# Bulk weights of the second layer through ScalarE's queue, late weights asked for two steps later, the first output tile's load three steps ahead, the keys' sums in another pool

## The chip, the core and the metric

One core of one Trainium2 chip runs the whole kernel. TensorE (PE) multiplies matrices; VectorE (DVE), ScalarE (ACT) and GpSimd (POOL) work on tiles in SBUF and read results from PSUM; SyncE (SP) does nothing but issue transfers. ScalarE can issue transfers too: SPq and ACTq in the profile are the two issuing queues. The metric is the device time of one execution in microseconds, the median of several.

## The reference

A prompt of 2048 tokens and a sample of 64 tokens go through two layers with 16 heads of 64. Layer A is softmax attention over a band of chunks, layer B is "stick-breaking" attention over a K/V pair that is projected from A's output. Cut to what matters:

```python
h = rms_norm(x, norm_a)
q, k, v, gate = split(h @ w_in_a, 4)
x = x + (band_attend(q, k, v, rel_bias) * silu(gate)) @ w_out_a     # layer A
k, v = split(rms_norm(x, norm_kv) @ w_kv, 2)                         # shared K/V
q, gate = split(rms_norm(x, norm_b) @ w_in_b, 2)
x = x + (sb_block(q, k, v) * silu(gate)) @ w_out_b                   # layer B
y = rms_norm(x, norm_f)

def sb_block(q, k, v):
    z = q @ k.T * SCALE
    log_fail = where(mask, log_sigmoid(-z), 0)
    later = suffix sums of log_fail, without the own place
    return where(mask, exp(log_sigmoid(z) + later), 0) @ v
```

Outputs are y for prompt and sample, and the new rows of K and V. Everything is f32.

## The kernel before, in words

To keep f32 accuracy, each operand is split into a high and a low part (names that end in h and l: `lwh`, `lwl`, `ph`, `pl`, `oh`, `ol`), and a product is two or three matmuls into one PSUM bank.

Each layer is a projection stage, bound by matmuls, and an attention stage. In the attention stage TensorE makes scores (`z`), transposes weights (`wt<-ident,s`) and multiplies by V (`acc<-ph,vt`, `acc<-pl,vt`); ScalarE makes exponentials and sigmoids (`f<-z`) and copies (`ph<-wt`), VectorE and GpSimd do the rest (`s`, `two`, `pl`). Results go to DRAM through `ot` (two buffers) as `o_a` and `o_b`.

Beside the attention, the class `Beat` puts in steps of other matrix work from a list, `beside`, at a rate of 0.4 (A) or 0.3 (B) steps a beat, so that TensorE has something to do while others work on the scores. The list holds, in order:

- late projections (`job_steps`, `late_job`): the second half's keys in layer A (8 jobs), the second half's gates (`w_bg`) and queries (`w_bq`) in layer B (16 jobs). A job has weights (`lwh`, `lwl`, from DRAM in layer B, where they were split before; in A split on the spot from `lraw`), eight products (`ps_j`, two chunks of four steps) and what follows: `sg` through ScalarE for gates, `sp` for queries and keys. For keys, `add_back` sums the two parts on GpSimd (`lkn<-sp`) and `token_rows` turns them for the output.
- `w_out_steps`, eight steps of one entry: layer A loads `woraw` and splits it into `big`; layer B loads the parts from DRAM, where they lie split (`parts`, 16 loads `big<-wo` of 512 KB).
- `out_steps`: output tiles of 128 tokens. Each loads `og` (o times gate) and `xr` (the residual), splits og into `oh` and `ol` in two cuts, and has eight products `ps_o`.

An entry is a triple: what to do ahead (loads, cuts), products, and what goes behind. `Beat.step` takes one product of the current entry per call. At an entry's first step it asks for the next entry's load; in the second half of the current entry it spreads the next entry's cuts. An entry whose load was not asked for waits nine beats after it (`ready`).

The order on an engine is Tile's scheduler's, except for what `in_place` pins: a pinned instruction stays behind the one traced before it on the same engine. Late weights, bulk weights and output tiles' loads are pinned. All transfers named here go through SyncE in the kernel before (`sp.dma_start`); ScalarE's queue carries loads of `wraw` and a few stores in the projection stages only. Transfers take eight completion semaphores in turn, over both queues, and an issue waits for the transfer eight issues earlier.

The pools that the change names: `lpool` and `rpool` lie on the two sides of SBUF, and a tile waits for the last readers of what lay in its place. `opool` has two buffers each of `oh` and `ol` (late weights and cuts share them), two of `xr` (also `sg` and `sp`), one of `og` (also `lraw`). PSUM tag `wt` (three banks) holds `wt` and `ps_j`.

In the profile almost every engine instruction has one line, that of the helper `traced` (L90), so instructions are told apart by their tiles.

Of the kernel before, what the change touches and what calls it, by code (L numbers as in the profile page):

```python
# [21 lines left out]
NP = 2048  # L22
# [26 lines left out]
HOLD = dict(a=1, b=2)  # L49

STEP = 2

SETTLE = 5
TOK = [(t * P, min(P, T - t * P)) for t in range((T + P - 1) // P)]
# [46 lines left out]
def encoder_step(ctx: ExitStack, tc: tile.TileContext, a: dict, o: dict):  # L101
# [634 lines left out]
    def late_job(L, kind, w, c0, g, hp, x2, first, prompt, rows_pool):  # L736
        st = {}

        def load():
            if L not in KEPT:  # L740
                st["raw"] = opool.tile([P, NK, P], F32, name="lraw", tag="og", bufs=1)
                c = c0 + hp * P
                sp.dma_start(st["raw"], w[:, c : c + P].rearrange("(k p) c -> p k c", p=P))
            st["wh"] = opool.tile([P, NK, P], F32R, name="lwh", tag="oh", bufs=2)
            st["wl"] = opool.tile([P, NK, P], F32R, name="lwl", tag="ol", bufs=2)
            if L in KEPT:
                for i, part in enumerate((st["wh"], st["wl"])):
                    sp.dma_start(f32(part), f32(lay[L]["w"][kind, hp][i]))

        def cut(k0):  # L750
            ks = slice(k0, k0 + STEP)
            scaled_split(st["wh"][:, ks], st["wl"][:, ks], st["raw"][:, ks], g[:, ks])

        def some(c, k0):
            if k0 == 0:
                st["ps"] = bank("ps_j")
            ps, wh, wl = st["ps"], st["wh"], st["wl"]
            cols = slice(c, c + CH)
            for k in range(k0, k0 + STEP):
                mm(ps, wh[:, k], x2[0][:, k, cols], start=(k == 0), stop=False)  # L760
                mm(ps, wh[:, k], x2[1][:, k, cols], start=False, stop=False)
                mm(ps, wl[:, k], x2[0][:, k, cols], start=False, stop=(k == NK - 1))

        def out(c):
            ps = st["ps"]
            at = slice(place(HALF + c), place(HALF + c) + CH)
            if kind == "g":
                sg = opool.tile([P, CH], F32, name="sg", tag="xr", bufs=2)
                act.activation(sg, ps, AF.Sigmoid)
                dve.tensor_tensor(sg, ps, sg, ALU.mult)  # L770
                queue.store(lay[L]["g"][hp][:, at], sg)
            else:
                sp = opool.tile([P, 2, CH], F32R, name="sp", tag="xr", bufs=2)
                split(sp[:, 0], sp[:, 1], ps)
                for s in range(2):
                    put(L, kind, hp, s, at, sp[:, s], queue.store)
                st[c] = sp
            if c + CH == HALF:
                done_late.add((L, kind, hp))

        def add_back(c):

            st["kn"] = rows_pool.tile([P, CH], F32, name="lkn", tag="lkn", bufs=1)
            gps.tensor_tensor(st["kn"], f32(st[c][:, 0]), f32(st[c][:, 1]), ALU.add)

        def token_rows(c):
            kn = st["kn"]
            ps = bank("ps_r")
            for j in range(4):
                flip(ps[:, j * P : j * P + P], kn[:, j * P : j * P + P])  # L790
            act.activation(kn, ps, AF.Copy)
            b = HALF + c - first
            dst = prompt[b : b + CH, hp * P : hp * P + P]
            queue.store(dst.rearrange("(j p) c -> p j c", p=P), kn.rearrange("p (j c) -> p j c", j=4))

        chunks = range(0, HALF, CH)
        behind = []
        for c in chunks:
            rows = kind == "k" and HALF + c >= first
            behind.append([partial(out, c)] + ([(2, partial(add_back, c)), (4, partial(token_rows, c))] if rows else []))  # L800
        products = [partial(some, c, k0) for c in chunks for k0 in range(0, NK, STEP)]
        cuts = [] if L in KEPT else [partial(cut, k0) for k0 in range(0, NK, STEP)]
        return [in_place(x) for x in [load] + cuts], products, behind

    def w_out_steps(src, w):

        raws = {}

        def parts(k):
            if k == 0:  # L810
                w.extend(big_pair())
            for i in range(2):
                sp.dma_start(f32(w[i][:, k]), f32(wod[k][:, i]))

        if src is None:
            return [([], [None], [[in_place(partial(parts, k))]]) for k in range(NK)]

        def load(k):
            if k < NK:
                tag = ("oh", "ol")[k % 2]  # L820
                raws[k] = opool.tile([P, D], F32, name="woraw", tag=tag, bufs=2)
                sp.dma_start(raws[k], src[k * P : (k + 1) * P])

        def cut(k):
            if k == 0:
                w.extend(big_pair())
            for c in range(0, D, CH):
                cols = slice(c, c + CH)
                split(w[0][:, k, cols], w[1][:, k, cols], raws[k][:, cols])
            del raws[k]  # L830

        return [
            (
                [in_place(partial(load, i)) for i in range(3)] if k == 0 else [],
                [None],
                [[in_place(partial(cut, k)), in_place(partial(load, k + 3))]],
            )
            for k in range(NK)
        ]
# [60 lines left out]
    class Beat:  # L900
# [4 lines left out]
        def __init__(self, lag, hold, scores_first, blank):  # L905
# [2 lines left out]
            self.clock = 0  # L908
            self.tiles, self.blocks, self.held, self.rests = [], [], [], []
            self.beside, self.rate, self.due = [], 0.0, 0.0  # L910
            self.now, self.at, self.ready, self.started = None, 0, 0, False
            self.steps, self.waiting = 0, []
            self.marks = []

# [9 lines left out]
        def step(self):  # L924


            if self.now is None:
                self.now, self.at = self.beside.pop(0), 0
                ahead = self.now[0]
                if ahead and not self.started:  # L930

                    ahead.pop(0)()
                    self.ready = self.clock + 9
                self.started = False
            if self.clock < self.ready:
                return 0.0
            ahead, products, behind = self.now
# [10 lines left out]
            n, rest = len(products), []  # L948
            half = max(n // 2, 1)
            following = self.beside[0][0] if self.beside else []  # L950
            if self.at == 0 and following:
                rest.append(following.pop(0))
                self.started = True
            self.at += 1
            if self.at % half == 0:
                for x in behind[self.at // half - 1]:
                    if type(x) is tuple:
                        self.waiting.append((self.steps + x[0], x[1]))
                    else:
                        rest.append(x)  # L960
            if self.at > half or n == 1:
                m = -(-len(following) // (n - self.at + 1))
                rest += [following.pop(0) for _ in range(m)]
            self.later(rest)
# [122 lines left out]
    with (  # L1087
# [8 lines left out]
        new = Sample("a", wpool)  # L1096
        w_out = []
        beat = Beat(LAG["a"], HOLD["a"], True, 1.0)
        beat.beside = job_steps("a", jobs_a, x2, NP - CACHE_A, o["a_k_p"], lpool)
        beat.beside += w_out_steps(a["w_out_a"][0], w_out)  # L1100
        order.on = False

# [161 lines left out]
    with (  # L1264
# [42 lines left out]
        new = Sample("b", wpool)  # L1307
        w_out = []
        beat = Beat(LAG["b"], HOLD["b"], False, 1.0)
        beat.beside = job_steps("b", jobs_b, x2, 0, o["b_k_p"], lpool)  # L1310
        beat.beside.insert(1, end_values())
        beat.beside += w_out_steps(None, w_out)
        order.on = False
# [235 lines left out]
```

## Time and profile before

| what | value |
|---|---|
| runs | 3270.53, 3279.95, 3283.12 us |
| median | 3279.95 us |
| profiled execution, own time | 3271.0 us |
| profiled execution, span | 3269.2 us |
| granted TensorE clock, mean | 0.996 |
| instructions | 53693 |
| DMA, moved over the span | 688.41 MB, 211 GB/s |

The span runs from the first to the last instruction; the execution's own time is 1.8 us longer. A row of a timeline has the start, the length, the engine, the line, the operation, its tiles (out<-in), their shapes and how many in a row, then in brackets the idle time of the engine before it and what ended that. PEld is TensorE's loading of the stationary operand, which lies beside the matmuls. A row of the windows has the busy time of each engine (and its instructions), then the granted clock (1.00 is full), the share of time in which the 16 DMA engines were busy (over 1 means that transfers overlap on them), and GB/s.

Layer A's attention runs from about 670 to 1420 us, layer B's from about 2030 us to the end. The late projections run at the start of each, `w_out_steps` of A around 980 to 1035 us, of B around 2650 to 2700 us.

### The profile page before, as it was taken

How to read it: one execution, taken by the hardware profiler on the slowest of the kernel's cores; microseconds unless marked ns; L12 is line 12 of the kernel's file. 1: busy time of each engine (PE TensorE's matmuls, PEld its weight loads, DVE VectorE, ACT ScalarE, POOL GpSimd, SP SyncE). 2: the span in 40 equal slices, each digit the busy share in tenths (PEclk: the TensorE clock that was granted, in tenths of full speed). 3: DMA queues.
4: the chain of work that ended last, by engine and by line, in shares of the span. 5: the costliest groups of instructions: out<-in, count | busy, mean ns of one | idle time of the engine just before them, and what ended most of it. 6: DMA issues, size and time to landing. Idle time of an engine off the chain costs nothing.

```text
span 3269.2 us, 53693 instructions
## 1 busy us (share of the span) xinstructions
PE 3198.9 (98%) x17928; PEld 2786.8 (85%) x17928; DVE 1882.2 (58%) x3786; ACT 1709.0 (52%) x3719; POOL 1291.7 (40%) x1950
## 2 busy tenths in 40 slices
PE   8999999999998999999999999999999989999999
PEld 7889999988887898878899999888888878888877
DVE  4235431147778776232044432888878878888873
ACT  5234222258888776143143442666666656666662
POOL 3001110025655554020044200444477767777761
PEclk9999999999999999999999999999999999999999
DMA  6359993387899983453399999977735575355423
GB/s 202 122 185 373 347 331 119 118 241 218 239 261 267 252 231 121 168 183 132 107 352 347 351 352 341 274 218 215 210 121 151 160 208 174 119 144 143 136 72 120
DMA packets 464891, 688.41 MB, mean 211 GB/s; under 512 B 51445, under 2 KB 261397, under 8 KB 464614
## 3 DMA queue, kind: packets, MB, share of 16 engines
q1 hardware_dynamic: 405158, 633.85, 62.1%
q10 hardware_dynamic: 59456, 51.13, 4.8%
q8 instruction: 143, 2.34, 0.3%
q14 instruction: 134, 1.10, 0.1%
HBM read 408.78 MB, written 276.07 MB: 209 GB/s over the span
## 4 chain that ended last, share of the span: by engine, by line
PE 77%; issue 7%; DVE 7%; DMA 4%; ACT 3%; POOL 2%; SPq 0%; POOLq 0%; ACTq 0%; DVEq 0%
PE ps_t L90 24%; PE ps_v L90 11%; PE acc L90 10%; PE z L90 9%; PE wt L90 9%; PE ps_j L90 7%; PE ps_o L90 5%; DVE s L90 3%; DVE pl L90 2%; PE ps_tr L90 1%; ACT ph L90 1%; DMA keys<-k_a 1%; ACT s L90 1%; DMA vt<-v_b 1%; PE ps_c L90 1%
## 5 line engine op out<-in xcount | busy, mean ns | idle before, releaser
L90 DVE TENSOR_TENSOR pl<-wt,ph 128x512 fp32r<-128x512 f32 (+1 forms) x864 | 552.4, 654 | 121.8 <-ACT ph L90 117.9
L90 ACT ACTIVATE ph<-wt 128x512 fp32r<-128x512 f32 (+1 forms) x864 | 485.5, 577 | 203.4 <-PE wt L90 181.9
L90 PE MATMUL ps_t<-x_own,wh 128*128 128x362 f32 (+1 forms) x2304 | 568.1, 327 | 0.0
L90 PE MATMUL wt<-ident,s 128*128 128x128 f32 x3472 | 550.6, 274 | 14.7 <-DVE pl L90 6.9
L90 PEld LDWEIGHTS wt<-ident,s 128*128 128x128 f32 x3472 | 417.2, 141 | 90.3 <-DVE pl L90 13.1
L90 ACT ACTIVATE f<-z 128x512 f32<-128x512 f32 (+4 forms) x680 | 355.0, 536 | 189.4 <-PE z L90 131.8
L90 PEld LDWEIGHTS ps_t<-x_own,wh 128*128 128x128 f32 x2304 | 405.4, 188 | 1.8
L90 POOL TENSOR_TENSOR s<-f,s 128x256 f32<-128x256 f32 x416 | 360.1, 867 | 104.0 <-DVE s L90 96.7
L90 PE MATMUL acc<-ph,vt 128*128 128x512 f32 (+3 forms) x1088 | 374.6, 379 | 17.8 <-ACT ot L90 8.6
L90 PE MATMUL z<-kt,q 128*128 128x512 f32 (+3 forms) x1280 | 373.6, 379 | 4.2 <-ACT f L90 2.7
L90 PE MATMUL ps_t<-x_own,wl 128*128 128x362 f32 (+1 forms) x1152 | 377.2, 328 | 0.0
L90 PE MATMUL acc<-pl,vt 128*128 128x512 f32 (+3 forms) x1088 | 363.3, 367 | 7.4 <-DVE pl L90 7.1
L90 POOL TENSOR_SCALAR s<-s,rc 128x640 f32<-128x640 f32 (+5 forms) x264 | 199.3, 759 | 387.8 <-DMA keys<-k_a 194.1
L90 PE MATMUL ps_o<-big,oh 128*128 128x512 f32 x1088 | 336.3, 393 | 0.0
L90 POOL TENSOR_TENSOR two<-f 128x256 f32<-128x256 f32 x416 | 258.7, 624 | 155.1 <-ACT f L90 139.8
L90 DVE TENSOR_TENSOR_SCAN s<-two,s,own 128x256 f32<-128x256 f32 x408 | 300.2, 739 | 34.2 <-POOL two L90 32.8
L90 PEld LDWEIGHTS z<-kt,q 128*128 128x128 f32 x1280 | 220.2, 190 | 33.8 <-ACT f L90 9.3
L90 PE MATMUL ps_j<-big,lwh 128*128 128x512 f32 x768 | 246.8, 397 | 1.5 <-DVE pl L90 0.6
L90 PE MATMUL ps_t<-big,wh 128*128 128x512 f32 x768 | 239.1, 392 | 0.0
L90 PEld LDWEIGHTS ps_o<-big,oh 128*128 128x128 f32 x1088 | 202.3, 188 | 40.9 <-ACT oh L90 0.2
L90 PEld LDWEIGHTS acc<-ph,vt 128*128 128x128 f32 x1088 | 197.4, 190 | 41.1 <-ACT ot L90 11.2
L90 DVE CUSTOM_DVE_ANT_0 s<-z,bias 128x640 f32<-128x640 f32 (+4 forms) x256 | 184.8, 733 | 78.5 <-PE wt L90 52.8
(148 smaller groups left out, 5526.7 us busy)
## 6 DMA issues: line engine op xcount, KB each, us to landing
vt<-v_b SPq DMA_DIRECT2D x80, 512.0 KB, 4.5
v_b<-vs SPq DMA_DIRECT2D x64, 512.0 KB, 5.9
q<-q_a SPq DMA_DIRECT2D x128, 256.0 KB, 5.9
q<-q_b SPq DMA_DIRECT2D x128, 256.0 KB, 4.3
vt<-v_a SPq DMA_DIRECT2D x48, 512.0 KB, 7.9
kt<-k_b SPq DMA_DIRECT2D x96, 256.0 KB, 5.6
keys<-k_a SPq DMA_DIRECT2D x80, 256.0 KB, 6.8
v_a<-vs ACTq DMA_DIRECT2D x32, 512.0 KB, 2.7
```

What stands on the lines that cost most here:

```text
L90: ins = op(*args, **kwargs)
```

## The change

Four edits:

1. The sums of the late keys (`lkn`) are allocated in `rpool` in place of `lpool`. Only layer A has them; in layer B the argument is without effect.
2. In layer B the loads of late weights (32) and of w_out's parts (16) are issued by ScalarE in place of SyncE.
3. An entry that has one thing to do ahead (layer B's late weights) is asked for at the third step of the entry before it (`BEHIND = 2`), in place of the first.
4. During `w_out_steps` (one product slot each), `step` looks up to three entries ahead for the first output tile and asks for its load then; where that tile is the very next entry, it waits nine beats and its cuts are not taken in at once. A name, `fetched`, holds which entry's load has been asked for, in place of the flag `started`.

```diff
+BEHIND = 2
...
             if L in KEPT:
                 for i, part in enumerate((st["wh"], st["wl"])):
-                    sp.dma_start(f32(part), f32(lay[L]["w"][kind, hp][i]))
+                    act.dma_start(f32(part), f32(lay[L]["w"][kind, hp][i]))
...
             for i in range(2):
-                sp.dma_start(f32(w[i][:, k]), f32(wod[k][:, i]))
+                act.dma_start(f32(w[i][:, k]), f32(wod[k][:, i]))
...
-                if ahead and not self.started:
+                if ahead and self.fetched is not ahead:
 
                     ahead.pop(0)()
                     self.ready = self.clock + 9
-                self.started = False
...
             following = self.beside[0][0] if self.beside else []
-            if self.at == 0 and following:
-                rest.append(following.pop(0))
-                self.started = True
+            coming = following
+            if n == 1:
+                coming = next((x[0] for x in self.beside[:3] if x[1] != [None]), [])
+            late = False
+            if coming and self.fetched is not coming and self.at == (BEHIND if n > 1 and len(coming) == 1 else 0):
+                rest.append(coming.pop(0))
+                self.fetched = coming
+                late = n == 1 and coming is following
+                if late:
+                    self.ready = self.clock + 9
...
-            if self.at > half or n == 1:
+            if self.at > half or n == 1 and not late:
...
-        beat.beside = job_steps("a", jobs_a, x2, NP - CACHE_A, o["a_k_p"], lpool)
+        beat.beside = job_steps("a", jobs_a, x2, NP - CACHE_A, o["a_k_p"], rpool)
...
-        beat.beside = job_steps("b", jobs_b, x2, 0, o["b_k_p"], lpool)
+        beat.beside = job_steps("b", jobs_b, x2, 0, o["b_k_p"], rpool)
```

How this moves instructions, at three places.

SyncE's queue, layer A, at the second half of the load of w_out (`woraw`). The names: `og` and `xr` are the first output tile's loads, `q`, `vt`, `gt` the attention's, `o_a` a store of its results. Before:

```order
L127 DMA o_a_109<-ot 128x512
L134 DMA gt<-gate_a_99 128x512
L134 DMA q<-q_a_82 64x2x512
L90 DMA woraw<-in_w_out_a 128x1024
L134 DMA q<-q_a_83 64x2x512 x2
L134 DMA vt<-v_a 128x4x256
L90 DMA woraw<-in_w_out_a 128x1024
```

and now:

```order
L128 DMA o_a_109<-ot 128x512
L135 DMA gt<-gate_a_99 128x512
L135 DMA q<-q_a_82 64x2x512
L91 DMA og<-o_a_107 128x8x128
L91 DMA xr<-in_x_prompt 128x1024
L91 DMA woraw<-in_w_out_a 128x1024
L135 DMA q<-q_a_83 64x2x512 x2
```

The two loads of the tile moved up by 22 rows, from behind a `vt` further down, past the second half of `woraw`, five loads of `vt` and the stores of `o_a_108`, `out_a_k_p` and `o_a_110`.

ScalarE, start of layer B's attention. The names: `lwh`/`lwl<-w_bq` are the second late job's weights, `<-w_bg_142` the third's, `sg` the first job's results (two chunks), `ends` a tile of the sample's, `f` scores. Before:

```order
L90 ACTIVATE kh<-ps_c 128x512
L90 ACTIVATE sh<-ps_t 128x362
L90 ACTIVATE kh<-ps_c 128x512
L90 ACT_TABLE_LOAD
L90 ACTIVATE sg<-ps_j 128x512 x2
L90 ACTIVATE ends<-ps_e 128x136
```

and now:

```order
L91 ACTIVATE sh<-ps_t 128x362
L91 DMA lwh<-w_bq_149 128x1024
L91 DMA lwl<-w_bq_149 128x1024
L91 ACTIVATE kh<-ps_c 128x512
L91 ACT_TABLE_LOAD
L91 ACTIVATE sg<-ps_j 128x512
L91 DMA lwh<-w_bg_142 128x1024
L91 DMA lwl<-w_bg_142 128x1024
L91 ACTIVATE sg<-ps_j 128x512
L91 ACTIVATE ends<-ps_e 128x136
```

The second job's weights now stand ahead of `kh`; the third's stand between the two `sg`.

SyncE, layer B, where the parts of w_out were loaded (`big`). Before:

```order
L90 DMA big_30644<-wo_165 128x1024
L90 DMA big_30645<-wo_165 128x1024
L90 DMA og<-o_b_137 128x8x128
L90 DMA xr<-x_158 128x1024
L134 DMA vt<-v_b 128x4x256
L90 DMA big_30644<-wo_166 128x1024
L90 DMA big_30645<-wo_166 128x1024
```

and now, the same place in the attention (`kt`, `q`, `vt` of the same block):

```order
L135 DMA kt<-k_b_122 64x2x512
L135 DMA vt<-v_b 128x4x256
L135 DMA kt<-k_b_122 64x2x512
L135 DMA q<-q_b_114 64x2x512
L135 DMA kt<-k_b_122 128x2x512
L135 DMA qs_21394<-q_b_116 64x2x64 x2
L135 DMA vt<-v_b 128x4x256 x5
```

The bulk loads have gone, and the first tile's `og` and `xr` stand earlier (behind the last stores of `q_b_118`'s first chunk and ahead of its second).

ScalarE, the same place now; before there was no DMA among these rows:

```order
L91 ACTIVATE otmp<-total_21401 64x64 x2
L91 DMA big_30644<-wo_160 128x1024
L91 DMA big_30645<-wo_160 128x1024
L91 ACTIVATE f<-z 128x512
L91 DMA big_30644<-wo_161 128x1024
L91 DMA big_30645<-wo_161 128x1024
L91 ACTIVATE ph<-wt 128x512 x3
L91 ACTIVATE f<-z 128x512 x2
L91 ACTIVATE ph<-wt 128x512
L91 ACTIVATE f<-z 128x512 x2
L91 DMA big_30644<-wo_162 128x1024
L91 DMA big_30645<-wo_162 128x1024
```

The pairs stand between ScalarE's `f` and `ph`, one pair for each step of `w_out_steps`.

More of the change, by code (lines that the diff above doesn't have):

```diff
@@ L910, in __init__ @@
             self.beside, self.rate, self.due = [], 0.0, 0.0
-            self.now, self.at, self.ready, self.started = None, 0, 0, False
+            self.now, self.at, self.ready, self.fetched = None, 0, 0, None
             self.steps, self.waiting = 0, []
```

## The prediction

> **What bounds the kernel now.** I read the page first: its busy shares, and the chain that ended last.
>
> ```profile
> span 3269.2 us, 53693 instructions
> PE 3198.9 (98%) x17928; PEld 2786.8 (85%) x17928; DVE 1882.2 (58%) x3786; ACT 1709.0 (52%) x3719; POOL 1291.7 (40%) x1950
> PE 77%; issue 7%; DVE 7%; DMA 4%; ACT 3%; POOL 2%; SPq 0%; POOLq 0%; ACTq 0%; DVEq 0%
> ```
>
> TensorE is busy for 3198.9 of 3269.2 us, and the change takes no matmul away. So all that it can win lies in 3269.2 − 3198.9 = 70.3 us of idle time, and in what the clock loses behind an idle stretch. The next view is therefore TensorE's waits, by what ended them (total, times, longest). I keep the rows that the change can touch.
>
> ```profile
> PE acc L90 <- ACT ot L90: 8.6, 4, 6.0
> PE acc L90 <- DMA vt<-v_b: 8.1, 2, 5.4
> PE wt L90 <- POOL s L90: 5.1, 4, 4.4
> PE z L90 <- ACT f L90: 2.7, 7, 1.0
> PE ps_j L90 <- DMA lwl<-w_bq: 1.2, 1, 1.2
> PE ps_j L90 <- DMA lwh<-w_bq: 0.5, 1, 0.5
> ```
>
> Five of the six are one long wait each with little beside it: single places, each with its own cause, and not a rate that runs through the kernel. So the work is to look at each place, and at what the change puts there.
>
> **The keys' sums.** The timelines of TensorE and GpSimd (start, length, instruction, idle time before it and its releaser), and the granted clock of that stretch:
>
> ```profile
> 695.82 1.42 PE L90 MATMUL z<-keys,q 128*128 128x320 f32 x8
> 701.64 0.44 PE L90 MATMUL wt<-ident,s 128*128 128x128 f32 x2 [4.41 <-POOL s L90]
> 702.39 1.94 PE L90 MATMUL z<-keys,q 128*128 128x320 f32 x7
> 699.55 1.26 POOL L90 TENSOR_TENSOR lkn<-sp 128x512 f32<-128x512 f32 x1 [6.01 <-DMA k_a<-sp]
> 700.79 2.35 POOL L90 TENSOR_SCALAR s<-s,rc 128x640 f32<-128x640 f32 x3
> 700.00:710.00 10.00, 8.36 (x44) 7.61 (x45) 5.60 (x19) 5.10 (x14) 5.54 (x7) 0.83 0.86 234
> ```
>
> GpSimd's first sum stood 6.01 us for a store to land, since its tile lay in memory that the store still read. The scaling of s is queued behind it, and TensorE waits for s. In the other pool only VectorE's half of sp is left to wait for, and GpSimd is free from 699.55 − 6.01 = 693.54. The sum then ends near 694.9 and the first s (2.35 / 3 = 0.8 us) is ready about when TensorE is done with the z that end at 697.2. All 4.41 us go. Behind the stall z went at 1.94 / 7 = 0.28 us against 1.42 / 8 = 0.18, and the window's clock is 0.83: 10 × 0.17 = 1.7 us at most, some of it in the idle time, so I count 1.1. Together **−5.5** (−6.1 to −4.4). Seven further sums run with no such wait and give nothing.
>
> **The first output tile's loads, layer A.** A step puts the loads of og and xr (512 KB each) ahead of the second half of the load of w_out, right behind the q<-q_a at 995.0, where SyncE had them at 1028.7. Here is what runs in between (start, length; for windows: busy time of PE, PEld, DVE, ACT, POOL, then clock, DMA share, GB/s):
>
> ```profile
> 995.02 0.58 SPq L134 DMA_DIRECT2D q<-q_a  x1
> 1009.64 1.06 SPq L127 DMA_DIRECT2D o_a<-ot  x1
> 1028.74 0.51 SPq L90 DMA_DIRECT2D og<-o_a  x1
> 1019.65 0.59 ACT L90 ACTIVATE ot<-acc 64x512 f32<-64x512 f32 x1 [6.36 <-DMA o_a<-ot]
> 1020.29 0.79 PE L90 MATMUL acc<-ph,vt 128*128 128x512 f32 x1 [6.01 <-ACT ot L90]
> 1010.00:1020.00 10.00, 3.74 (x24) 2.82 (x22) 4.84 (x12) 3.25 (x8) 1.12 (x2) 0.83 1.04 346
> ```
>
> The store o_a<-ot, issued at 1009.6, lands only at 1019.6 behind DMA engines that are full (share 1.04). ScalarE waits for its buffer, TensorE waits for ScalarE for 6.01 us. The change adds 1.05 MB ahead of that store; at the 346 GB/s of the window it takes 1.05 / 0.346 = 3.0 us. It takes them out of a later stretch where no wait of TensorE's hangs on a load, so nothing comes back. **+3** (0, if the queue drains before 1009, to +4 with the clock). The edit's aim, an og that is there early, is worth nothing here: no wait of TensorE's for og or oh is in the list.
>
> **Late weights of layer B.** There are 32 loads, two for each of 16 jobs. They leave SyncE's queue for ScalarE's, and are asked for at a job's third step. At the stage's start:
>
> ```profile
> 2032.25 0.70 PE L90 MATMUL ps_j<-big,lwh 128*128 128x512 f32 x2 [0.52 <-DMA lwh<-w_bq]
> 2034.12 0.80 PE L90 MATMUL ps_j<-big,lwl 128*128 128x512 f32 x1 [1.16 <-DMA lwl<-w_bq]
> 2040.62 0.62 PE L90 MATMUL ps_j<-big,lwh 128*128 128x512 f32 x2
> 2019.61 0.60 ACT L90 ACTIVATE kh<-ps_c 128x512 fp32r<-128x512 f32 x1 [0.87 <-PE ps_c L90]
> 2025.08 0.60 ACT L90 ACTIVATE sg<-ps_j 128x512 f32<-128x512 f32 x1 [3.58 <-PE ps_j L90]
> 2031.12 0.60 ACT L90 ACTIVATE sg<-ps_j 128x512 f32<-128x512 f32 x1 [5.43 <-PE ps_e L90]
> 2025.03 0.50 SPq L90 DMA_DIRECT2D lwh<-w_bq  x1
> 2038.34 0.32 SPq L90 DMA_DIRECT2D lwh<-w_bg  x1
> 2039.36 0.32 SPq L90 DMA_DIRECT2D lwl<-w_bg  x1
> 2030.00:2040.00 10.00, 8.32 (x37) 6.27 (x36) 0.69 (x1) 0.60 (x1) 0.00 (x0) 0.83 1.08 288
> ```
>
> SyncE issued lwh<-w_bq at 2025.0 behind a row of K and V loads; on ScalarE it stands right ahead of this kh, before 2019.6, so it is there in time: 0.52 + 1.16 = 1.7 us of idle time go, and with clock 0.83 some 1.5 us more. But the next pair, lwh and lwl<-w_bg, now stands on ScalarE between the two sg. The program's DMAs take eight completion semaphores in turn, over both queues, and an issue waits until the DMA eight before it has landed; on SyncE this pair could go at 2038.34 and 2039.36 for that reason. The second sg stands behind it: ready at 2031, done near 2040.3. TensorE needs the bank that it frees for the job's second half, at 2040.62 before and some 3.2 us earlier now: 2040.3 − 2037.4 = 2.9 us of new wait, and 1.7 with the clock. −3.2 + 4.6 = **+1.4** (−3.2, if those two land sooner, to +3).
>
> The other 14 pairs cost ScalarE its time to issue, for which the nearest row is the loads that it issues already (ns: least, median, most):
>
> ```profile
> L379 ACTq DMA_DIRECT2D wraw<-in_w_in_b x16: 374/376/437, 1754.3 to 1973.9; - x16
> ```
>
> 28 × 0.376 = 10.5 us of ScalarE's queue, in a stage in which TensorE waits for f only seven times (2.7 us in all) among 680. So most of a 0.75 us delay is taken up by scores that are ready ahead; I take a quarter, **+2.6** (0 to +10.5). No wait for a late weight stood there before, so nothing is won.
>
> **Bulk weights of layer B's w_out.** 16 loads of 512 KB leave SyncE for ScalarE.
>
> ```profile
> 2671.96 3.44 SPq L90 DMA_DIRECT2D xr<-x  x1
> 2675.50 1.82 SPq L134 DMA_DIRECT2D vt<-v_b  x1
> 2678.28 0.73 PE L90 MATMUL z<-kt,q 128*128 128x512 f32 x2 [0.98 <-ACT f L90]
> 2684.39 0.80 PE L90 MATMUL acc<-ph,vt 128*128 128x512 f32 x1 [5.37 <-DMA vt<-v_b]
> 2693.99 0.50 PE L90 MATMUL acc<-ph,vt 128*128 128x512 f32 x1 [2.76 <-DMA vt<-v_b]
> 2680.00:2690.00 10.00, 5.62 (x23) 4.99 (x24) 4.25 (x8) 3.45 (x7) 4.63 (x10) 0.66 1.06 317
> vt<-v_b SPq DMA_DIRECT2D x80, 512.0 KB, 4.5
> big<-wo SPq DMA_DIRECT2D x16, 512.0 KB, 9.0
> ```
>
> The load vt<-v_b, issued at 2675.5 behind bulk loads, og and xr, took 8.9 us to its use, against a median of 4.5. With the bulk loads on ScalarE, spread by its own instructions over 2670 to 2713, SyncE asks for vt several us earlier and fewer bytes are in flight. Both waits for vt and the one for f should go: 5.37 + 2.76 + 0.98 = 9.1 us, and about 2 us of clock (0.66 in the window, half of it in the idle time). Against it stand 16 × 0.376 = 6.0 us of issues on a busy ScalarE; a third on the path is 2. **−9** (−11 to 0, if vt stays as late as it is).
>
> **Sum:** −5.5 + 3 + 1.4 + 2.6 − 9 = −7.5 us on the profiled 3271.0 us (its span and 1.8 around it). The bounds add up to −20 and +13. The median of the runs shown is 3279.95, with 3270.53 the fastest; the profiled execution lies at the lower end. I apply the difference to the middle of the two, (3271.0 + 3279.95) / 2 = 3275.5: **3268**. What a measurement tells from no change is 0.5%, 16.4 us: faster means under 3263.5, slower over 3296.4.
>
> **Rivals.**
> *All touched waits go.* The 21.2 us of the rows with brackets above (4.41 + 6.01 + 1.68 + 9.1), and some 7 us of clock, ScalarE's issues being covered: −28, 3247.5. For it: each wait has one cause. Against: the store in layer A gets more in front of it, not less. Chance 0.15.
> *The bulk loads are only moved.* DMA shares of 1.04 to 1.08 say that the engines, not a queue, are full; then vt waits as long as before, the −9 becomes +2, and the sum is +3.5: 3279. For it: the window 2680 to 2690 at 1.06. Against: 2675.5, the late issue of vt, is the queue's doing. The Trainium skill, "DMA: Bandwidth & Descriptors", section "Issuing engines are not separate DMA queues", says that DMAs from several engines run on the same 16 DMA engines, and that a second issuer saves only the time of issuing. That is this rival's rule, and the full windows agree with it so far. Chance 0.22.
> *ScalarE is blocked at the bulk loads: slower.* Bulk loads took 9.0 us to land; eight pairs in 2670 to 2713 come every 5.4 us. If each pair's wait for an earlier landing holds ScalarE 9.0 − 5.4 = 3.6 us, and TensorE with it, that is 29 us, and 1.5 us of clock behind each, 12; less the 11 regained, +30, with the other terms +31: 3307. It decides once a landing takes longer than the distance of the pairs by more than TensorE's lead. For it: SyncE's xr issue above took 3.44 us, a wait of just this kind, and on ScalarE f and ph stand behind it. Against: with the pairs spread out fewer transfers are in flight. The Trainium skill, the same page, section "Anatomy of one DMA — SWDGE (gpsimd) path", has it that DMA engines do not wait on semaphores, and that any such wait sits on the issuing sequencer; the xr row agrees. Chance 0.06.
> *The sum's tile waits after all,* for another reader of its new place: 5.5 us less won, 3273.5. Chance 0.07.
>
> **How the numbers follow.** The forecast has 0.50. Its own width (bounds −20 to +13 about 3275.5: 3255 to 3288) holds the second and the fourth rival too; I give 3254 to 3288, which leaves out most of the first and the third, some 0.2. Faster by over 0.5%: nearly all of the first rival, 0.14, and a quarter of the forecast, whose middle lies 4.5 us above the bound: 0.27. Slower: 0.05 of the third. Within: 0.68.
>
> **What would show it.** Right: GpSimd's first lkn starts near 693.6 with no idle time that k_a<-sp ends; no wait of TensorE's for vt<-v_b; a wait for ot near 1015 of about 9 us; near 2037 a wait of TensorE's that a ScalarE sg ends; ScalarE's queue with lwh and lwl at about 0.37 us. Wrong: the wait for ot shorter than 6 us, ScalarE idle before f behind a big<-wo, or TensorE's waits for f well above 2.7 us over layer B.

## The result, and the profile after

The changed kernel takes 3264.76 us, the median of 8 runs (3261.26 to 3268.9); the kernel before, on the same chip, 3273.01 us (8 runs, 3270.53 to 3283.12). The ratio is 0.9969, with a 95% interval of 0.9959 to 0.9979: faster by 0.31%, within the half per cent that was set as no change. The medians differ by 8.3 us, where 7.5 was forecast. The profiled execution's own time is 3263.8 us.

Two rows of the page after:

```profile
span 3262.0 us, 53645 instructions
PE 3197.6 (98%) x17928; PEld 2783.9 (85%) x17928; DVE 1885.5 (58%) x3786; ACT 1709.4 (52%) x3719; POOL 1289.7 (40%) x1950
```

and TensorE's waits in it (total, times, longest):

```profile
PE acc L91 <- ACT ot L91: 9.0, 4, 6.5
PE ps_j L91 <- DVE sg L91: 7.0, 1, 7.0
PE z L91 <- ACT f L91: 2.6, 7, 0.8
PE wt L91 <- POOL s L91: 0.8, 3, 0.3
```

The waits for vt, lwh and lwl have left the list, that for s fell from 5.1 to 0.8, that for f stayed. One stands there that was not there before: 7.0 us for sg. The wait for ot is half a us longer.

To see where the time went, each matmul of the one profile is set beside the same one of the other (same tiles, same number in order). The table gives how far TensorE's starts lie ahead (−) or behind, as the median in stretches that end a part's place, for the kernel after and for the experiments below; then TensorE's idle time in gaps over 0.15 us, summed over the five places. A column's difference from the one before it is what lies between. The stretches are the same for all, though the profiles shift by some us against them: a gap of 1.5 us near 990 us counts in 990–1045 for before, p2, p3 and p4 alone, so that before's 10.7 compares with after's 10.1 as 9.2.

| profile | 720–980 | 1050–1100 | 1900–2010 | 2100–2150 | 2600–2655 | 2740–2800 | idle 690–720 | 990–1045 | 2010–2110 | 2110–2655 | 2655–2730 |
|---|---|---|---|---|---|---|---|---|---|---|---|
| before | | | | | | | 4.4 | 10.7 | 5.3 | 3.6 | 9.6 |
| after | −5.2 | −3.3 | −3.5 | +1.0 | +1.7 | −7.3 | 0 | 10.1 | 8.7 | 5.0 | 2.4 |
| p1 sums alone | −5.7 | −8.0 | −7.2 | −6.5 | −6.5 | −5.3 | 0 | 6.5 | 4.9 | 3.6 | 8.9 |
| p2 bulk alone | +1.2 | +0.8 | +0.3 | +6.8 | +7.0 | −0.7 | 5.0 | 9.7 | 9.0 | 3.5 | 3.3 |
| p3 late alone | +0.4 | −0.7 | −0.8 | +3.1 | +4.6 | +5.7 | 4.4 | 8.7 | 8.3 | 5.3 | 10.5 |
| p4 ahead alone | −1.5 | −0.2 | +0.8 | +4.0 | +4.1 | +4.4 | 3.6 | 11.0 | 6.9 | 3.6 | 10.0 |
| q1 late back | −5.3 | −4.7 | −4.1 | −3.2 | −2.3 | −10.8 | 0 | 10.1 | 5.0 | 3.9 | 3.0 |
| q2 and ahead in B only | −2.7 | −4.6 | −3.0 | −2.4 | −2.4 | −10.8 | 1.6 | 6.9 | 5.3 | 3.5 | 3.0 |
| q3 first two on ACT | −5.5 | −7.5 | −7.0 | −2.8 | −2.1 | −10.7 | 0 | 6.7 | 8.0 | 4.0 | 2.8 |
| q4 all but third on ACT | −5.1 | −8.0 | −7.8 | −4.5 | −3.8 | −12.5 | 0 | 6.0 | 7.7 | 5.0 | 2.6 |
| r1 bulk on POOL | −3.3 | −1.0 | −0.7 | −0.7 | +0.1 | +31.4 | 1.0 | 10.8 | 5.0 | 3.9 | 21.2 |
| r2 half of the bulk | −5.1 | −7.2 | −6.5 | −0.9 | 0.0 | +7.0 | 0 | 6.9 | 7.3 | 3.9 | 13.4 |
| r3 no early tile | −4.7 | −8.1 | −7.2 | −5.2 | −4.4 | −12.3 | 0 | 5.9 | 6.3 | 4.0 | 2.9 |
| r4 woraw on ACT | −4.6 | −2.4 | −2.1 | −1.0 | −0.1 | −8.6 | 0.9 | 6.2 | 6.8 | 3.9 | 2.9 |

One thing must be kept in mind with it: a wait that a landing ends varies between executions of the same code. Near 2078 us TensorE waited 0.7 to 4.4 us for q or gs in nine profiles whose code there is that of before, and in before itself 1.1 us, for `ph` (p2's +6.8 in the fourth column comes in good part from there: it has before's code up to 2650 us). So a single difference of a few us at such a place proves little; the columns have to be read down.

The rows of the kernel after at the four places. The keys' sums, on GpSimd and TensorE:

```profile
693.62 1.29 POOL L91 TENSOR_TENSOR lkn<-sp 128x512 f32<-128x512 f32 x1
696.45 0.80 POOL L91 TENSOR_SCALAR s<-s,rc 128x640 f32<-128x640 f32 x1 [1.53 <-DVE rc L91]
695.81 1.42 PE L91 MATMUL z<-keys,q 128*128 128x320 f32 x8
697.31 0.44 PE L91 MATMUL wt<-ident,s 128*128 128x128 f32 x2
```

The sum starts at 693.6 with no idle time before it, and TensorE goes from z to wt without a gap. Layer A's store of o_a (ScalarE, TensorE):

```profile
1015.37 0.59 ACT L91 ACTIVATE ot<-acc 64x512 f32<-64x512 f32 x1 [6.65 <-DMA o_a<-ot]
1016.02 0.80 PE L91 MATMUL acc<-ph,vt 128*128 128x512 f32 x1 [6.45 <-ACT ot L91]
```

and its window, where the clock was 0.83 before:

```profile
1010.00:1020.00 10.00, 3.98 (x12) 3.55 (x13) 2.29 (x7) 4.63 (x10) 2.94 (x5) 0.60 0.88 277
```

What the store hung on shows in SyncE's queue (the first row is of before, whose store went at 1009.64; the other two are of after):

```profile
998.56 0.33 SPq L90 DMA_DIRECT2D woraw<-in_w_out_a  x1
996.94 0.33 SPq L91 DMA_DIRECT2D woraw<-in_w_out_a  x1
1005.94 1.12 SPq L128 DMA_DIRECT2D o_a<-ot  x1
```

These two loads of `woraw` are the transfers eight issues ahead of the store. By the trace they landed at 1009.58 and 1005.87, and the store went 0.06 and 0.07 us later: the turn of the eight semaphores held it until then. From its issue to ScalarE's `ot` it was 10.0 us before and 9.4 after.

Layer B's start (TensorE, ScalarE's queue, ScalarE):

```profile
2040.32 1.22 PE L91 MATMUL ps_j<-big,lwh 128*128 128x512 f32 x2 [6.98 <-DVE sg L91]
2036.19 0.33 ACTq L91 DMA_DIRECT2D lwh<-w_bg  x1
2038.57 0.33 ACTq L91 DMA_DIRECT2D lwl<-w_bg  x1
2038.94 0.60 ACT L91 ACTIVATE sg<-ps_j 128x512 f32<-128x512 f32 x1 [17.13 <-DMA q<-q_b]
```

and its window:

```profile
2035.00:2045.00 10.00, 4.68 (x11) 3.72 (x12) 1.83 (x6) 1.33 (x4) 0.82 (x2) 0.55 1.03 308
```

The pair stands ahead of the second sg and is let go at 2036.2 and 2038.6; sg, its sum on VectorE and TensorE follow at once. The clock falls to 0.55 behind it. The place of the bulk loads (TensorE, ScalarE's queue):

```profile
2680.96 0.73 PE L91 MATMUL z<-kt,q 128*128 128x512 f32 x2 [0.80 <-ACT f L91]
2679.07 0.86 ACTq L91 DMA_DIRECT2D big<-wo  x2
2685.64 1.75 ACTq L91 DMA_DIRECT2D big<-wo  x2
```

its window, and the median time of a bulk load to its landing (9.0 before):

```profile
2680.00:2690.00 10.00, 8.02 (x44) 5.85 (x43) 8.21 (x14) 6.75 (x14) 8.72 (x19) 1.00 1.06 363
```

```profile
big<-wo ACTq DMA_DIRECT2D x16, 512.0 KB, 7.0
```

The DMA engines are as full as before (1.06 in the same window), yet TensorE has 8.02 us busy in place of 5.62, at full clock.

### The profile page after: what moved, and what is told of

Read it like the earlier page. It is cut to its first block, busy times and chain, and to the rows that moved or that the text cites. A ratio compares the mean times of both kernels' runs of the same rounds, so it can differ in the third digit from the quotient of the medians.

```text
span 3262.0 us, 53645 instructions
## 1 busy us (share of the span) xinstructions
PE 3197.6 (98%) x17928; PEld 2783.9 (85%) x17928; DVE 1885.5 (58%) x3786; ACT 1709.4 (52%) x3719; POOL 1289.7 (40%) x1950
## 4 chain that ended last, share of the span: by engine, by line
PE 79%; issue 7%; DVE 7%; DMA 3%; ACT 2%; POOL 1%; SPq 0%; ACTq 0%; POOLq 0%; DVEq 0%
PE ps_t L91 24%; PE ps_v L91 11%; PE acc L91 11%; PE z L91 10%; PE wt L91 9%; PE ps_j L91 7%; PE ps_o L91 5%; DVE s L91 3%; DVE pl L91 2%; PE ps_tr L91 1%; DMA woraw<-in_w_out_a 1%; ACT ph L91 1%; PE ps_c L91 1%; POOL s L91 0%; PE ps_n L91 0%
## 5 line engine op out<-in xcount | busy, mean ns | idle before, releaser
L91 PEld LDWEIGHTS acc<-pl,vt 128*128 128x128 f32 x1088 | 193.6, 190 | 41.0 <-DVE pl L91 25.7
```

Source lines behind the costliest of these rows:

```text
L91: ins = op(*args, **kwargs)
```

## The experiments

The first four are the kernel before with one part of the change each; before was 3275.59 us beside them. Each of the three groups ran on a chip of its own, so between groups the ratios are to be compared, not the times.

**p1: the keys' sums alone.** In the kernel before, only:

```diff
-        beat.beside = job_steps("a", jobs_a, x2, NP - CACHE_A, o["a_k_p"], lpool)
+        beat.beside = job_steps("a", jobs_a, x2, NP - CACHE_A, o["a_k_p"], rpool)
```

> The kernel before with the keys' sums in the other pool and nothing else. Theory (the four parts add up): GpSimd's first sum starts near 693.6 us, TensorE's 4.41 us wait for s goes with its slow clock, and TensorE is 5.2 us ahead from 710 us to the end, about 3268 where before is 3273. Rival (the gain came from the SyncE queue or from what the other parts moved): TensorE's wait for s stays near 4 us and the time is that of before.

Measured: 3266.38 us, ratio 0.9981 (0.9972 to 0.9990). No gap between 690 and 720, TensorE 5.7 us ahead behind it. The part is worth its 5.2 to 5.7 us by itself. (Not in every profile: in q2 and r1, where TensorE waits for `ph` 1.6 and 1.0 us near 703, the lead behind it is 2.7 and 3.3 us.) In this profile the wait for ot near 1010 us was also shorter (3.4 us), which gave 2.3 us more.

**p2: the bulk loads alone.**

```diff
             for i in range(2):
-                sp.dma_start(f32(w[i][:, k]), f32(wod[k][:, i]))
+                act.dma_start(f32(w[i][:, k]), f32(wod[k][:, i]))
```

> The kernel before with only the 16 bulk loads of layer B's w_out on ScalarE's queue; the output tile's og and xr are asked for where they were. Theory (SyncE's queue held vt back): both waits of TensorE for vt go, TensorE is 9 us ahead from 2700 us on, and ScalarE's f waits no longer than before. Rival 1 (it was the earlier og and xr that freed SyncE's queue): less than half of the 9 us, with a wait for vt left of some 3 to 5 us. Rival 2 (the transfers are only moved, the DMA engines being full): no change.

Measured: 3268.41 us, ratio 0.9977 (0.9968 to 0.9986). TensorE's idle time at 2655 to 2730 is 3.3 us in place of 9.6, and it gains 7.7 us between the columns 2600 and 2740; no wait for vt is left. Its waits for f:

```profile
PE z L91 <- ACT f L91: 2.5, 8, 0.8
```

and the window of the old stall (TensorE 5.62 us busy before):

```profile
2680.00:2690.00 10.00, 8.80 (x56) 7.14 (x55) 9.06 (x16) 6.51 (x14) 9.42 (x19) 1.00 1.06 383
```

Both rivals fall: the early tile is not needed for it, and full DMA engines do not hinder it.

**p3: the late weights alone.**

```diff
+BEHIND = 2
...
-                    sp.dma_start(f32(part), f32(lay[L]["w"][kind, hp][i]))
+                    act.dma_start(f32(part), f32(lay[L]["w"][kind, hp][i]))
```

and the third edit's condition in `step`.

> The kernel before with only the late weights of layer B on ScalarE's queue, asked for at the third step. Theory (the loads ahead of the pair land when the full DMA engines let them, whatever TensorE does, so each us by which TensorE comes earlier is a us more of waiting): without the 3.5 us gained upstream, TensorE reaches the job's second half 3.5 us later and waits 3 to 4 us there in place of 7.0; from 2060 us on the kernel is 1 to 2 us behind before, in place of the 5.3 us that the part cost in the full change. Rival (the cost is the part's own and does not depend on what came before): 5 us behind, with a wait of 7 us.

Measured: 3278.14 us, ratio 1.0008 (0.9999 to 1.0017). TensorE and ScalarE's queue:

```profile
2042.26 1.22 PE L91 MATMUL ps_j<-big,lwh 128*128 128x512 f32 x2 [5.93 <-DVE sg L91]
2038.28 0.33 ACTq L91 DMA_DIRECT2D lwh<-w_bg  x1
2040.51 0.33 ACTq L91 DMA_DIRECT2D lwl<-w_bg  x1
2045.37 0.28 ACT L91 ACTIVATE ends<-ps_e 128x136 f32<-128x136 f32 x1 [3.89 <-DMA k_b<-kl]
```

The theory falls, and the rival is nearer. The wait is 5.9 us, with nothing gained upstream. Both issues come 2 us later than in the kernel after (2036.19 and 2038.57 there), and the stage itself starts later by 2.7 (its last projection matmul at 2017.1 against 2014.4): the landings move with the stage, and 1.0 us of the wait at most came from upstream.

**p4: the early tile alone.**

```diff
+            if n == 1:
+                coming = next((x[0] for x in self.beside[:3] if x[1] != [None]), [])
```

with the rest of the fourth edit.

> The kernel before with only the first output tile's load asked for up to three steps ahead, in both layers. Theory: layer A loses about 2 us near 1015 to 1040 us (more bytes ahead of the store of o_a that ScalarE waits for), layer B gains 0 to 3 us (vt no longer stands behind og and xr, but still behind the bulk loads); in all within 3 us of before. Rival (the earlier og and xr are what took the 9 us of layer B's waits for vt away): 6 to 7 us faster.

Measured: 3277.43 us, ratio 1.0005 (0.9996 to 1.0014). The waits for vt are all there, and the longest for ot is 6.0 us, as it was before:

```profile
PE acc L91 <- DMA vt<-v_b: 8.6, 2, 5.9
PE acc L91 <- ACT ot L91: 8.5, 4, 6.0
```

Between the columns 2600 and 2740 it gains nothing (+4.1 to +4.4). So the rival falls; the early tile has no part in layer B's gain.

The next four take the changed kernel and undo parts; before was 3273.43 us beside them.

**q1: late weights back on SyncE**, asked for at the first step (`BEHIND = 0`, `sp.dma_start`).

> The full change with the late weights of layer B back on SyncE's queue and asked for at the first step. Theory (that part costs nothing or a little on the whole: its new wait of 6 to 7 us at the second sg stands against the waits for lwh, lwl and for q and gs near 2078 us that it takes away): no wait of TensorE's for sg, waits of 2 to 3 us for lwh and lwl and of 1 to 4 us near 2078 us instead; 0 to 3 us faster than the full change. Rival (the part costs the 5.3 us by which the two first profiles differ there): 5 us faster than the full change.

Measured: 3264.85 us, ratio 0.9968 (0.9956 to 0.9981), as the full change (0.9969). The wait for sg is gone, lwh and lwl are waited for again (1.2 and 1.4 us), q near 2076 us for 0.9 us. Read down the table: idle time at 2010 to 2110 is 5.3, 4.9, 9.0, 6.9, 5.0, 5.3, 5.0, 7.3, 6.3 and 6.8 us in the ten profiles with these weights on SyncE, 6.2 in the mean, and 8.7, 8.3, 8.0 and 7.7 in the four with some of them on ScalarE, 8.2. By that the part costs some 2 us there, not 5.3, though the two ranges overlap: the profile of before was at the low end of its own spread.

**q2: and the early tile in layer B alone.**

```diff
-            if n == 1:
+            if n == 1 and not self.scores_first:
...
-                late = n == 1 and coming is following
+                late = n == 1 and not self.scores_first and coming is following
```

> As the kernel with the late weights back on SyncE, and the first output tile asked for ahead in layer B alone. Theory (1 MB ahead of the store of o_a lengthens ScalarE's wait for it): TensorE's wait for ot near 1010 us is 3.4 to 5.5 us, as in the four profiles without the early load (6.0, 3.4, 5.1, 4.1), not 6 to 6.5 as in the two with it (6.5, 6.0); 1 to 2 us faster than with it. Rival (that wait only varies from run to run): no difference, the wait is again above 5.9 us.

Measured: 3260.95 us, ratio 0.9959 (0.9946 to 0.9971). The longest wait for ot is in these rows, q1's first:

```profile
PE acc L91 <- ACT ot L91: 8.9, 4, 6.5
```

```profile
PE acc L91 <- ACT ot L91: 5.8, 5, 2.7
```

With the early loads the wait was 6.5, 6.0 and 6.5 us (after, p4, q1). Without them and with the sums moved it was 3.4, 2.7, 2.5, 2.9, 3.7 and 2.6 (p1, q2, q3, q4, r2, r3), but 7.6 in r1; with the sums where they were, 6.0, 5.1 and 4.1 (before, p2, p3). With the sums moved that is 6.5 against 3.6 us in the mean, r1 speaking against; with the sums where they were, 6.0 against 5.1. So early loads seem to lengthen it by 1 to 3 us; 3264.85 against 3260.95 us agrees, though the two intervals overlap.

The theory's way is not what the traces show: the store does not take longer. From its issue to ScalarE's `ot` it was 9.4, 9.2 and 9.8 us with early loads (after, p4, q1), and 9.1 to 10.5 in the ten others without r4. It is issued later: 3.6 to 4.0 us ahead of TensorE's stall with early loads, 4.6 to 7.6 without, but 3.6 in r1. In all thirteen it went within 0.1 us of the landing of the load of `woraw` eight issues ahead of it, and with early loads og and xr stand ahead of that load.

**q3: only the first two jobs' weights on ScalarE**, the others on SyncE, at the third step; the rest as q2.

```diff
-                    act.dma_start(f32(part), f32(lay[L]["w"][kind, hp][i]))
+                    (act if hp == 0 else sp).dma_start(f32(part), f32(lay[L]["w"][kind, hp][i]))
```

> As the kernel before this one, but the weights of the first two late jobs (gate and query of the first pair of heads) through ScalarE's queue and the other fourteen through SyncE's, asked for at the third step. Theory (what costs is only the third job's pair, queued on ScalarE between the two sg behind transfers that have not landed): neither the waits for lwh and lwl nor that for sg is left; 2 to 4 us faster than with all late weights on SyncE. Rival (any of these loads on ScalarE holds something there, or another wait comes in its place, as for a bank that sg frees later anyway): a wait of 3 us or more is left between 2020 and 2050 us.

Measured: 3260.45 us, ratio 0.9956 (0.9942 to 0.9969). Neither lwh, lwl nor sg is waited for, but other waits came (ScalarE, then TensorE):

```profile
2024.75 0.60 ACT L91 ACTIVATE sg<-ps_j 128x512 f32<-128x512 f32 x1 [5.44 <-PE ps_e L91]
2038.11 0.28 ACT L91 ACTIVATE ends<-ps_e 128x136 f32<-128x136 f32 x1 [12.77 <-DMA k_b<-kl]
2038.62 1.08 PE L91 MATMUL z<-kt,q 128*128 128x384 f32 x4 [2.29 <-ACT f L91]
```

Another wait came in their place, as the rival has it, though at 2.3 us it is under the 3 us that the rival names; the theory's gain of 2 to 4 us did not come. ScalarE's first f stands behind `ends`, and `ends` waits for a landing, here that of the store k_b<-kl. Measured from the stage's last projection matmul, `ends` came 25.9 to 27.1 us later in all ten profiles with the weights on SyncE, 27.2 and 27.4 in q3 and q4, 28.2 and 29.3 with all of them on ScalarE. (In four of the ten the profile names the load lwh<-w_bg in place of the store.) In q3 that landing is what TensorE meets next: its idle time from 2020 to 2050 is 4.0 us, against 3.5 in q2, which waits for lwh and lwl. So the 1.7 us for lwh and lwl that I counted as a gain were cover: without them TensorE is out of work earlier.

**q4: all but the third job's weights on ScalarE.**

```diff
+                    (sp if (kind, hp) == ("g", 1) else act).dma_start(f32(part), f32(lay[L]["w"][kind, hp][i]))
```

> As the kernel before this one, but only the third job's weights go through SyncE's queue, all fifteen others through ScalarE's. Theory (ScalarE's scores are ready ahead, so 0.75 us of issuing per job is covered): between 2110 and 2650 us TensorE loses no more than 2 us against the kernel with two jobs on ScalarE; idle time there 4 to 5 us against 3.6. Rival (the price that I had put on it, a quarter of the issuing time): 2.5 us or more lost there.

Measured: 3260.37 us, ratio 0.9955 (0.9943 to 0.9968). Idle time at 2110 to 2655 is 5.0 us, 5.0 and 5.3 in the other two with these loads on ScalarE, and 3.5 to 4.0 in the eleven without. Issuing costs 1.3 us of idle time; between the columns it costs 0.7 (−4.5 to −3.8), as q3 loses too. The theory holds.

The last four ask what it was about ScalarE's queue that helped; before was 3276.24 us. All have the late weights on SyncE; r1, r2 and r4 are q2 with one more edit.

**r1: bulk loads through GpSimd's queue** (`gps.dma_start`).

> As the kernel with the late weights back and the early tile load in layer B alone (about 3261 us), but the 16 bulk loads go through GpSimd's queue in place of ScalarE's. Theory (what counts is that the bulk loads no longer stand on SyncE ahead of vt, and are asked for one pair at a step): no wait of TensorE's for vt either, 0 to 4 us slower than with ScalarE for GpSimd's longer issuing. Rival (ScalarE's waits pace the loads, and that is what helps): waits for vt of 3 us or more come back.

Measured: 3299.87 us, ratio 1.0072 (1.0056 to 1.0087): slower than before. No wait for vt came back, but GpSimd stood still between the two issues of a pair:

```profile
2668.55 0.79 POOL L91 DMA_DIRECT2D big<-wo  x1
2675.46 0.55 POOL L91 DMA_DIRECT2D big<-wo  x1 [6.13 <-issue]
2682.06 0.60 POOL L91 DMA_DIRECT2D big<-wo  x1 [0.57 <-issue]
2686.27 0.53 POOL L91 DMA_DIRECT2D big<-wo  x1 [3.62 <-issue]
```

and TensorE waited for it:

```profile
PE wt L91 <- POOL s L91: 14.2, 8, 5.4
```

Idle time of TensorE at 2655 to 2730 went to 21.2 us. vt is freed by GpSimd's queue too, as the theory has it, but the price is the issuing engine's; I had put it at 0 to 4 us, and it was some 40 (+31.3 between the columns, −8.4 in q2). The profile names nothing for those 3.6 to 6.1 us, but by the trace the second load of each of the eight pairs went 0.31 to 0.32 us after the first had landed (2675.46 after 2675.14). Why it waits so is open. GpSimd's loads also have eight semaphores of their own, so that no issue of SyncE's or ScalarE's waits for them.

**r2: only the high halves on ScalarE.**

```diff
-                act.dma_start(f32(w[i][:, k]), f32(wod[k][:, i]))
+                (act, sp)[i].dma_start(f32(w[i][:, k]), f32(wod[k][:, i]))
```

> As the same kernel, but only the high halves of the bulk weights go through ScalarE's queue, the low halves through SyncE's, where the program puts them ahead of vt again (five of eight). Theory (vt is late by the bytes asked for ahead of it): half as many bytes, TensorE waits for vt 2 to 5 us in place of 8, and the kernel is 2 to 5 us slower than with all on ScalarE. Rival (any number of bulk loads moved off SyncE does): no wait for vt.

Measured: 3275.95 us, ratio 0.9994 (0.9985 to 1.0003): the whole gain is gone; against q2's 0.9959 it is 0.35% slower, 11 us. No wait for vt is left, but the theory's dose can't be read from that: TensorE stands 9.6 us for something else there, in which vt lands. In its place, on ScalarE, its queue and SyncE's:

```profile
2669.73 0.38 ACT L91 ACTIVATE pp<-wt 128x256 fp32r<-128x256 f32 x1
2680.17 0.35 ACTq L91 DMA_DIRECT2D big<-wo  x1
2680.56 0.60 ACT L91 ACTIVATE f<-z 128x512 f32<-128x512 f32 x1 [10.45 <-DMA big<-wo]
2664.90 1.63 SPq L91 DMA_DIRECT2D big<-wo  x3
```

and on TensorE:

```profile
PE z L91 <- ACT f L91: 11.9, 9, 9.6
```

ScalarE's first bulk load waits 10 us for a bulk load to land, one of SyncE's, since the eight semaphores go round over both queues, and f behind it waits too. This is the mechanism of the prediction's third rival: TensorE idles 9.6 us for f. In the changed kernel the first bulk load on ScalarE had no bulk load ahead of it in either queue, and the waits for f stayed at 2.6 us.

**r3: no early tile in either layer** (the lines of the fourth edit out): the sums moved, the bulk loads on ScalarE, nothing else.

> The keys' sums moved and the bulk loads on ScalarE, late weights on SyncE as before, and no early tile load in either layer. Theory (asking for the first tile early is worth nothing in layer B, since nothing of TensorE's waited for og, and with the bulk loads gone vt is not held back by og and xr either): the same time as with the early load in layer B, within 2 us, and the same idle time of 2.5 to 3.5 us between 2655 and 2730. Rival (og and xr ahead of vt cost): a wait for vt of 1 to 3 us.

Measured: 3259.0 us, ratio 0.9951 (0.9938 to 0.9963), the fastest with r4; idle time at 2655 to 2730 is 2.9 us, no wait for vt. The early tile is worth nothing in layer B. Two of the four edits make the whole gain: against the full change, the ratio is 0.9951 / 0.9969 = 0.9982, some 6 us, though the two intervals overlap.

**r4: layer A's loads of w_out through ScalarE too.**

```diff
-                sp.dma_start(raws[k], src[k * P : (k + 1) * P])
+                act.dma_start(raws[k], src[k * P : (k + 1) * P])
```

> As the kernel with the late weights back and the early tile load in layer B alone, and layer A's eight loads of w_out go through ScalarE's queue too. Theory (there the store of o_a is issued in time and lands late, since the DMA engines are full; another queue for the weights takes no byte away): TensorE's wait for ot near 1010 us stays at 2 to 4 us, as in three profiles without the edit (2.7, 2.5, 2.9). Rival (a second queue helps wherever bulk loads stand beside the attention's): the wait goes below 1 us.

Measured: 3260.35 us, ratio 0.9951 (0.9937 to 0.9964). The theory falls for the wait: TensorE waited for ot 0.5 and 1.1 us there. Nor does its ground hold, that the store is issued in time: in the three profiles named it was held until a load of `woraw` had landed (see q2). The time moved little all the same, since ScalarE now waits with its loads (ScalarE's queue, ScalarE, TensorE):

```profile
968.79 0.34 ACTq L91 DMA_DIRECT2D woraw<-in_w_out_a  x1
969.22 1.09 ACT L91 ACTIVATE ph<-wt 128x512 fp32r<-128x512 f32 x2 [3.14 <-DMA woraw<-in_w_out_a]
969.87 0.50 PE L91 MATMUL acc<-ph,vt 128*128 128x256 f32 x2 [2.31 <-ACT ph L91]
```

A wait of 2.3 us at 967 and one of 1.2 at 989 took its place. How much of the shorter wait is due to the loads' later places and how much to the queue was not tried.

## Why the prediction came out

The terms, in us, as forecast and as measured in the profiles (differences between columns of the table; the runs that bear on each in brackets):

| term | forecast | measured |
|---|---|---|
| keys' sums | −5.5 | −5.2 after (p1 −5.7, q2 −2.7) |
| early tile, layer A | +3 | +1.9 after (p4 +1.3); the wait some 1 to 3 us longer over all profiles (6.5 and 2.7 in q1 and q2) |
| late weights, layer B's start | +1.4 | +4.5 after (p3 +3.9); about +2 over all profiles |
| late weights, later on | +2.6 | +0.7 after (p3 +1.5, q4 +0.7; but q3 +0.7 too, with most of these loads on SyncE) |
| bulk loads | −9 | −9.0 after (p2 −7.7, q1 to q4 −8.4 to −8.7) |
| sum | −7.5 | −7.3 in the last column (−0.2 lies between the places) |

That the sum is met so closely is luck in part: the errors of the terms (+0.3, −1.1, +3.1, −1.9 and 0 us) nearly cancel.

**Right, by the steps given.** The two gains are the two waits that were named, each at its size with the clock behind it, and each alone gives its gain. The absolute 3268 was 3 us high, mostly since the 3275.5 that it started from lay 2.5 us above the median of eight.

**Near in size, wrong in the way: the early tile, layer A.** The prediction has the store issued at 1009.6 and landing 3.0 us later for the bytes ahead of it, with a wait of about 9 us as the sign. The wait was 6.5 us, and the store took 9.4 us in place of 10.0. What the loads put off was its issue, which waits for a load of `woraw` that og and xr now precede (q2). That +1.9 lies near +3 is luck.

**Wrong: the price at layer B's start.** The step that failed is "ready at 2031, done near 2040.3 … 2040.3 − 2037.4 = 2.9 us of new wait". The wait was 7.0 us, and 5.9 alone. I took the landings of vt and q from before (2038.3 and 2039.4, 20.4 and 21.5 us behind the stage's last projection matmul at 2017.9). But the same edit puts the second job's weights, 1.05 MB, ahead of them; in the kernel after the two issues that wait for them came 21.8 and 24.2 us behind it, 1.4 and 2.7 us later. That these bytes are the cause is likely, not shown: in the ten profiles with the weights on SyncE the two issues lie at 19.8 to 21.9 and 21.0 to 23.1 us. I had charged bytes ahead in layer A and not here. And I set TensorE's time by the clock of before, though it comes 3.5 us earlier; the wait should have been worked out from the stage's own start. The gain that I set against it, 1.7 us and its clock, was none: q3 shows TensorE held by the landing of k_b<-kl where lwh and lwl do not hold it. That the part's cost over all profiles is near the +1.4 is luck, two errors of opposite sign.

**Mis-sized: the issues on ScalarE.** A quarter of 10.5 us was put on the path; 0.7 us came in after and q4, 1.5 in p3, and 0.7 in q3 as well. In the bulk loads' place the third that was charged (2 us) may be nearer: p2 and q1 to q4 leave 2.6 to 3.3 us of idle time at 2655 to 2730.

**The rivals.** That all touched waits go fell: the wait for ot stayed (6.5) and a new one came. That the bulk loads are only moved fell with p2: the DMA share in the window stayed at 1.06, and the wait went. The Trainium skill's rule ("DMA: Bandwidth & Descriptors", "Issuing engines are not separate DMA queues") agrees with that share, which did not move, but not with what TensorE gained, if only the issuing time is saved: 16 issues at about 0.4 us are 6 us, and TensorE gained 7.7 to 9.0 net. What changed is the order: bulk loads later and one pair at a time, vt no longer behind them. Before, each of SyncE's issues from 2659.6 to 2672.0 went within 0.1 us of the landing of the transfer eight issues ahead of it; in the kernel after, its five loads of vt from 2665.2 to 2676.5 went 0.2 to 4.5 us behind that landing, so that it held none of them back for long. That ScalarE is blocked hardly happened here (in the row 2685.64 the second issue stood 1.1 us), and did in r2; the row with 10.45 us agrees with the Trainium skill, same page, "Anatomy of one DMA — SWDGE (gpsimd) path", that such a wait sits on the issuing sequencer. The row on which the prediction rests this rival was misread: the transfer eight issues ahead of xr landed at 2671.95, just before the row begins, so that SyncE's wait of this kind is the 1.9 us ahead of it, and what the 3.44 us of the issue itself are the trace does not show. That the sums wait after all fell with the row at 693.62.

**Left open.** Whether the bulk loads, asked for as late on SyncE's own queue as they are on ScalarE's, would do the same was not tried: r1 shows that ScalarE is not needed to free vt, but not that another queue is.

## What to carry to other kernels

Where loads for later work stand in one queue ahead of a load that is waited for, moving them can pay even on full DMA engines, because it changes the order; but look at what stands behind each moved issue on its new engine, and which transfers that issue must wait for: the same move gave −9 us with all 16 loads on ScalarE, +7 with 8 of them, and +31 on GpSimd. When an edit asks for bytes earlier, charge them to every transfer behind them, at each place, and work out new waits from the stage's own start. Before a stall is counted as a gain, find the next thing that its engine will meet: if that is a landing, the stall was cover.

## What the runs showed of the hardware that was not expected

- Waits that end with a landing differ between executions of one code far more than compute does: 0.7 to 4.4 us near 2078 us, 2.5 to 7.6 us for ot near 1010 us without early loads, while TensorE's lead changes by only 0.1 to 1.6 us over the 800 us from 1100 to 1900, in all thirteen profiles.
- Two 512 KB loads issued one behind the other by GpSimd lay 4.2 to 6.9 us apart (2668.55 to 2675.46, 2682.06 to 2686.27); the second went 0.31 to 0.32 us after the first had landed, in all eight pairs. On ScalarE's queue the two lay 0.36 or 0.37 us apart in seven of eight pairs.
- With eight semaphores in turn, a store's issue can hang on a load that has nothing to do with it: in thirteen profiles the store of o_a went within 0.1 us of the landing of the load of `woraw` eight issues ahead.
- ScalarE's issue of a late weight took 0.33 us for the first of a pair and mostly 0.33 to 0.50 for the second: 0.39 in the mean, near the 0.376 us of the loads that it issued before.
